# The last unit of a mixture-of-experts kernel holds two experts instead of one

## The chip, the cores and the metric

The kernel runs on one core of a Trainium2 chip. The metric is the device time of one execution in microseconds; the median of several runs counts.

## The reference

One decoder layer on 256 tokens of 1024 channels, all float32. First a token mixer (sparse attention and an mLSTM branch) with a residual and a LayerNorm, then a mixture of 16 experts, again with a residual and a LayerNorm. The change is in the experts:

```
def hier_moe(x, w_grp, b_grp, w_rt, b_rt, w_gate, w_up, w_down):
    t = x.reshape(-1, D)                                   # 256 x 1024
    ...                                                    # top group, then top 2 experts in it
    combine = ...                                          # 256 x 16, two nonzero weights per token
    out = jnp.zeros_like(t)
    for e in range(N_EXPERTS):                             # 16 experts
        hdn = jax.nn.silu(t @ w_gate[e]) * (t @ w_up[e])   # 1024 -> 512
        out = out + combine[:, e:e + 1] * (hdn @ w_down[e])  # 512 -> 1024
    return out.reshape(B, S, D)
```

## The kernel before

Up to about 228 us the kernel computes the token mixer, the first LayerNorm and the routing. Then come the experts, in seven units. The weights of an expert are 6 MB (gate, up and down, two halves of 1 MB each), 96 MB for all, and each is read once from HBM.

**Slots and units.** An expert does not compute all 256 tokens, only the tokens sent to it, up to a cap. Four experts have fixed slots with 64 columns each (`NSTAT`, `CAP`). The other twelve are sorted by their token counts on the chip, and `PLAN` (L30) gives their slots the widths 128; 64, 64; four times 32; four times 32; 32. A unit is one tuple of `PLAN`, 128 token rows in all, and `ORDER` (L31) is the order in which the units run after the two fixed ones: (64, 64), (32 x 4), (128), (32 x 4), (32). So the fifth unit is the expert with 128 columns, the sixth has four experts of 32 columns, and the seventh, the last one, has one expert of 32 columns (`ALONE`, L32). An expert with more tokens than its cap is finished by `beyond` (L1314), a branch with a loop that runs only if the counts ask for it.

**One unit.** `onehot` (L1093) builds a 0/1 matrix from tokens to columns for two units at once. `gather` (L1115) multiplies the normalised tokens, kept as a high and a low part in float32r, by it: for each of 8 chunks of channels four products with 128x128 stationary tokens and the one-hot as the moving operand, 256 columns for two units, 32 for the last one. `scaled` (L1110) takes the result out on ScalarE and VectorE. `back` (L1134) transposes the one-hot for the way back and picks the combine weights `cw`. `gate` (L1171), `up_h` (L1184) and `down` (L1236) are the three matrix products; the tokens are stationary, the weights move, 512 columns at a time. Where a unit has several experts, their columns lie in different column tiles of TensorE (`slots`, L1126: 2 x 64 or 4 x 32 columns), and the products of the experts run beside one another. A plain float32 product is two records in the trace, a float32r product is one. `hidden_T` (L1195) transposes the hidden values, `combine` (L1250) multiplies by the transposed one-hot and adds to `acc`.

**The last unit before.** Its one expert has 32 columns, so `product_alone` (L1151) puts four chunks of the contraction into the four column tiles, two deep, and a product with `fold` (a matrix that adds the four 32-row blocks and copies the sum to all four) gives the whole sum. `hidden_T` with `fold` does this for up. `down_part` (L1207) again has one quarter of the contraction in each column tile, one deep; the combine adds the four. The output columns are done in three parts (`CUTS`: 512, 320 and 192), and the last down half is loaded in the two smaller pieces (`late`).

**Order.** The main loop (L1410) emits for the third and the fifth unit: one-hot for two units, combine of an earlier unit, `back`, down product of the unit before, gather, gate, up, combine of the unit before; for the units between, which share that gather: `back`, gate, down product of the unit before, up. For the last unit it is: combine, `beyond`, one-hot, `back`, gather, down product of the sixth unit, gate, up, combine of the sixth unit, tail. A framework turns this into one program per engine; it moves independent instructions against one another, but not past the branch of `beyond`.

**Loads.** All weight loads stand in one list (`loads_in_order`, L302) in the order in which the units use them (for the last unit: down of the sixth, gate, up, down), and SP issues them in this order (`load`, L128). A load needs a free place of the ring `we`; `consumed` (L67) gives places back when a product has read them.

Of the kernel before, what the change touches and what calls it, by code (L numbers as in the profile page):

```python
# [17 lines left out]
P = 128  # L18
D = 1024
KC = D // P  # L20
S = 256
# [38 lines left out]
def tile_layer(ctx: ExitStack, tc: tile.TileContext, x, w_in, cst, rows, toep, w_uk, w_uv,  # L60
# [1072 lines left out]

    def back(OH, u, unit):  # L1134

        cm = unit[4]
        us = slice(u * P, (u + 1) * P)
        pt = tp_tile("poht")
        for b in range(NB):
            nc.tensor.transpose(pt[:, b * P:(b + 1) * P], OH[:, b, us].bitcast(F32), ident)  # L1140
        OHT = wk.tile([P, S], F32R, tag="sc", name="oht", bufs=2)
        nc.scalar.copy(OHT, pt[:, :S])  # L1142
        pc = sm_tile("pcw")
        for b in range(NB):
            nc.tensor.matmul(pc[:, 0:len(unit[1])], OH[:, b, us].bitcast(F32), cm[:, b, :], start=b == 0, stop=b == 1)
        cw = wk.tile([P, 1], F32, tag="cw", name="cw", bufs=2)
        for i, ss, _ in ((0, slice(0, P), {}),) if unit[2] == ALONE else slots(unit):
# [23 lines left out]
    def gate(unit, u, psg=None):  # L1171
        if unit[2] == ALONE:
            part = wk.tile([P, 512], F32, tag="w2", name="part", bufs=2)
            nc.scalar.copy(part, product_alone(unit, 0))
# [5 lines left out]
        sg = wk.tile([P, 512], F32, tag="w2", name="sg", bufs=2)  # L1180
        nc.scalar.activation(sg, psg, AF.Silu)
        return sg

    def up_h(unit, u, sg, cw):  # L1184
        if unit[2] == ALONE:
            psu = product_alone(unit, 1)
# [3 lines left out]
        h = wk.tile([P, 4, P], F32, tag="w2b", name="h", bufs=2)  # L1190
        nc.vector.scalar_tensor_tensor(h.rearrange("p j q -> p q j"), psu.rearrange("p (q j) -> p q j", j=4), cw[:, 0:1],  # L1191
# [3 lines left out]
    def hidden_T(h, alone=False):  # L1195
        pt = tp_tile("pht").rearrange("p (j t) -> p j t", j=4)
        for j in range(4):
            if alone:

                nc.tensor.matmul(pt[:, j, :], h[:, j, :], fold, start=True, stop=True)  # L1200
            else:
                nc.tensor.transpose(pt[:, j, :], h[:, j, :], ident)
        hT = wk.tile([P, 4, P], F32, tag="hT", name="hT")
# [3 lines left out]
    def down_part(unit, hT, y, c0, n):  # L1207
# [12 lines left out]
    def y_parts(y, psd, c0, n):  # L1220
        ys = slice(c0, c0 + n)
        nc.scalar.copy(y[:, 0, ys], psd)  # L1222
        nc.vector.tensor_tensor(y[:, 1, ys], psd, y[:, 0, ys].bitcast(F32), op=ALU.subtract)  # L1223
# [12 lines left out]
    def down(unit, h):  # L1236
        hT, y = hidden_T(h), y_tile()
# [76 lines left out]
    def beyond():  # L1314

        assert not pend
        n_more = nc.values_load(nex[0:1, 0:1], min_val=0, max_val=2 * NE, skip_runtime_bounds_check_because="a sum of counts")
        item = wk.tile([P, 1], F32, tag="nmx", name="item")
        nc.gpsimd.memset(item, 0.0)
        with tc.If(n_more > 0):  # L1320
            with tc.For_i(0, n_more, 1):
# [31 lines left out]
                nc.vector.tensor_scalar(item, item, 1.0, None, op0=ALU.add)  # L1353

# [5 lines left out]
    def others():  # L1360
# [39 lines left out]
        fold_xg = wk.tile([P, P + KC * 32], F32, tag="wrs", name="fold_xg")  # L1400
        fold = fold_xg[:, :P]
        xga = fold_xg[:, P:].rearrange("p (k t) -> p k t", k=KC)
        nc.vector.tensor_reduce(fold[:, 0:32], ident.rearrange("p (i s) -> p s i", i=4), AX.X, ALU.add)
        nc.vector.tensor_copy(fold[:, 32:].rearrange("p (i s) -> p i s", i=3), fold[:, 0:32].unsqueeze(1).to_broadcast([P, 3, 32]))
        return fold, xga
# [4 lines left out]
    for n in range(NUNITS):  # L1410
        unit = units[n]
        if waits:
            if unit[2] == ALONE:
# [3 lines left out]
            if unit[2] != ALONE:  # L1417
                combine(*waits)
        OHT, cw = back(OH, n % 2, unit)
        if waits and unit[2] == ALONE:  # L1420
            gather(OH, 32, xg=xga)
        if waits:
            y = down(*prev[:2])
            if unit[2] != ALONE:
                gather(OH, 2 * P)
# [3 lines left out]
        if n == 1:  # L1429
            fold, xga = others()  # L1430
# [102 lines left out]
```

## Time and profile before

| | |
|---|---|
| median of 3 runs | 445.21 us (442.96 to 446.66) |
| the profiled execution | 442.91 us |
| its span, first to last instruction | 441.2 us |
| granted TensorE clock, mean | 0.974 |
| busy: TensorE, VectorE, ScalarE, GpSimd | 95%, 51%, 37%, 10% |
| read from HBM | 135.74 MB, 310 GB/s over the span |

The profiled execution is 1.7 us longer than its span. Busy shares are means over stages with different limits: the mixer with many small steps, and the experts with TensorE and the DMA engines both busy. In the trace PE is a matrix product on TensorE and PEld its weight load, DVE is VectorE, ACT is ScalarE, POOL is GpSimd, SPq is the queue of the engine that issues the loads. `psg`, `psu`, `pp` and `psd` are the results of gate, up, the last unit's gate and up, and down; `pxg` is the gather; `poht` and `pht` are transposes, `pcomb` the combine.

### The profile page before, as it was taken

How to read it: one execution, taken by the hardware profiler on the slowest of the kernel's cores; microseconds unless marked ns; L12 is line 12 of the kernel's file. 1: busy time of each engine (PE TensorE's matmuls, PEld its weight loads, DVE VectorE, ACT ScalarE, POOL GpSimd, SP SyncE). 2: the span in 40 equal slices, each digit the busy share in tenths (PEclk: the TensorE clock that was granted, in tenths of full speed). 3: DMA queues.
4: the chain of work that ended last, by engine and by line, in shares of the span. 5: the costliest groups of instructions: out<-in, count | busy, mean ns of one | idle time of the engine just before them, and what ended most of it. 6: DMA issues, size and time to landing. Idle time of an engine off the chain costs nothing.

```text
span 441.2 us, 7257 instructions
## 1 busy us (share of the span) xinstructions
PE 417.0 (95%) x2832; PEld 300.9 (68%) x2832; DVE 226.1 (51%) x493; ACT 163.3 (37%) x294; POOL 45.4 (10%) x74
## 2 busy tenths in 40 slices
PE   6999999999999999999999999999998999979980
PEld 6999996999999999999974345443334444436340
DVE  3698996499656755686573118214031212221247
ACT  4558556766766444455465020210112100101210
POOL 6325305031011001110000000000000000000001
PEclk9999999999999999999999999999999999995995
DMA  8982770797296788659697999999999999999972
GB/s 254 340 271 83 282 247 4 232 377 231 113 362 215 283 271 302 190 179 386 229 352 284 359 424 420 403 377 426 422 420 423 418 424 420 423 419 420 415 253 95
DMA packets 48518, 137.28 MB, mean 311 GB/s; under 512 B 3538, under 2 KB 32354, under 8 KB 36450
## 3 DMA queue, kind: packets, MB, share of 16 engines
q1 hardware_dynamic: 47394, 135.75, 81.1%
q10 hardware_dynamic: 1088, 1.05, 0.8%
q8 instruction: 23, 0.38, 0.4%
q14 instruction: 13, 0.11, 0.1%
HBM read 135.74 MB, written 1.05 MB: 310 GB/s over the span
## 4 chain that ended last, share of the span: by engine, by line
PE 80%; DMA 10%; DVE 5%; ACT 3%; issue 1%; SPq 0%; POOL 0%; DVEq 0%; ACTq 0%
PE psg L1166 10%; PE psu L1166 9%; PE psd L1243 7%; PE accT L253 7%; PE accT L249 7%; PE accT L252 7%; DMA we<-in_w_gate_dram 4%; DMA we<-in_w_down_dram 4%; PE pcomb L1229 3%; PE pxg L1121 2%; PE accY L249 2%; PE accZ L249 2%; PE accK L249 2%; PE accK L252 2%; PE accK L253 2%; PE accZ L253 2%
## 5 line engine op out<-in xcount | busy, mean ns | idle before, releaser
L249 PE MATMUL accT<-xh,split 128*128 128x256 f32 (+1 forms) x264 | 75.6, 286 | 0.0
L253 PE MATMUL accT<-xh,split 128*128 128x256 f32 (+1 forms) x264 | 75.1, 284 | 0.3 <-DVE split L240 0.3
L252 PE MATMUL accT<-xl,split 128*128 128x256 f32 (+1 forms) x264 | 75.1, 284 | 0.0
L240 DVE TENSOR_TENSOR split<-raw,split 128x1024 fp32r<-128x1024 f32 (+2 forms) x52 | 63.9, 1234 | 18.5 <-ACT split L239 18.3
L239 ACT CAST split<-raw 128x1024 fp32r<-128x1024 f32 (+2 forms) x59 | 59.3, 1013 | 32.4 <-PE accT L253 9.8
L1243 PE MATMUL psd<-we,hT 128*32 128x512 f32 (+2 forms) x240 | 48.6, 634 | 1.9 <-ACT hT L1204 1.9
L253 PEld LDWEIGHTS accT<-xh,split 128*128 128x128 f32 (+1 forms) x264 | 50.1, 190 | 0.5 <-DVE split L240 0.5
L249 PEld LDWEIGHTS accT<-xh,split 128*128 128x128 f32 (+1 forms) x264 | 50.1, 190 | 0.4 <-PE pl L589 0.2
L252 PEld LDWEIGHTS accT<-xl,split 128*128 128x128 f32 (+1 forms) x264 | 50.1, 190 | 0.0
L1166 PE MATMUL psu<-we,xg 128*32 128x512 f32 (+2 forms) x240 | 47.5, 594 | 0.0
L1166 PE MATMUL psg<-we,xg 128*32 128x512 f32 (+2 forms) x232 | 45.8, 595 | 0.0
L1223 DVE TENSOR_TENSOR y<-psd,y 128x512 fp32r<-128x512 f32 x12 | 8.3, 692 | 64.6 <-ACT y L1222 64.6
L1243 PEld LDWEIGHTS psd<-we,hT 128*32 128x32 f32 (+2 forms) x240 | 15.5, 131 | 30.4 <-issue 25.3
L1166 PEld LDWEIGHTS psu<-we,xg 128*32 128x32 f32 (+2 forms) x240 | 15.2, 126 | 26.7 <-issue 26.4
L1166 PEld LDWEIGHTS psg<-we,xg 128*32 128x32 f32 (+2 forms) x232 | 13.9, 125 | 24.4 <-issue 22.6
L1191 DVE SCALAR_TENSOR_TENSOR h<-psu,cw,sg 128x512 f32<-128x512 f32 x6 | 6.7, 1120 | 46.1 <-PE psu L1166 33.5
L1472 POOL TENSOR_TENSOR nm<-nm,nhalf 128x2 f32<-128x2 f32 x1 | 1.8, 1771 | 209.5 <-DVE nm L1473 209.5
L1222 ACT CAST y<-psd 128x512 fp32r<-128x512 f32 x12 | 7.0, 586 | 40.6 <-PE psd L1243 40.6
L1230 DVE TENSOR_TENSOR x<-x,pcomb 128x512 f32<-128x512 f32 (+2 forms) x30 | 17.9, 645 | 7.4 <-PE pcomb L1229 7.3
L1142 ACT CAST oht<-poht 128x256 fp32r<-128x256 f32 x7 | 2.6, 372 | 50.6 <-PE pcomb L1229 32.0
L240 POOL TENSOR_TENSOR split<-raw,split 128x1024 fp32r<-128x1024 f32 x7 | 17.5, 2501 | 20.1 <-ACT split L239 19.9
L1229 PE MATMUL pcomb<-y,oht 128*128 128x512 f32 (+2 forms) x60 | 18.6, 436 | 0.2 <-ACT y L1217 0.2
(356 smaller groups left out, 811.3 us busy)
## 6 DMA issues: line engine op xcount, KB each, us to landing
we<-in_w_up_dram SPq DMA_DIRECT2D x32, 1024.0 KB, 10.1
we<-in_w_gate_dram SPq DMA_DIRECT2D x31, 1024.0 KB, 9.5
we<-in_w_down_dram SPq DMA_DIRECT2D x31, 1024.0 KB, 13.5
raw<-in_w_in_dram SPq DMA_DIRECT2D x18, 1024.0 KB, 6.9
raw<-in_w_out_dram SPq DMA_DIRECT2D x4, 1024.0 KB, 4.9
raw<-in_w_up_a_dram SPq DMA_DIRECT2D x2, 1024.0 KB
raw<-in_w_up_m_dram SPq DMA_DIRECT2D x2, 1024.0 KB, 6.0
raw<-in_w_in_dram SPq DMA_DIRECT2D x2, 528.0 KB
```

The lines of the kernel that those rows point to most:

```text
L239: a = nc.scalar.copy(hi, raw)
L240: b = (nc.gpsimd if pool else nc.vector).tensor_tensor(lo, raw, hi.bitcast(F32), op=ALU.subtract)
L249: i = nc.tensor.matmul(o, ah, bh, start=start, stop=False)
L252: nc.tensor.matmul(o, ah, bl, start=False, stop=False)
L253: return nc.tensor.matmul(o, al, bh, start=False, stop=stop)
L1121: nc.tensor.matmul(ps[:, k, :n], part[:, b, (k0 + k) * P:(k0 + k + 1) * P], OH[:, b, :n], start=i == 0, stop=i == 3)
L1166: last = nc.tensor.matmul(ps[ss, :], xg[:, kc, u * P + ss.start:u * P + ss.stop], wtiles[unit[0], wi, i, hf][kc % 4], start=kc == 0, stop= ...
L1222: nc.scalar.copy(y[:, 0, ys], psd)
L1223: nc.vector.tensor_tensor(y[:, 1, ys], psd, y[:, 0, ys].bitcast(F32), op=ALU.subtract)
L1229: i = [nc.tensor.matmul(pc, o, v, start=i == 0, stop=i == len(parts) - 1) for i, (o, v) in enumerate(parts)]
L1230: nc.vector.tensor_tensor(acc[:, b, ys], acc[:, b, ys], pc, op=ALU.add)
L1243: nc.tensor.matmul(psd[nh][ss, :], hT[:, j, ss], wtiles[unit[0], 2, i, hf][j % 2][:, nh * 512:nh * 512 + 512], start=j == 0, stop=j == 3, ...
```

## The change

`PLAN` becomes 128; 64, 64; four times 32; three times 32; 32, 32. The caps of the twelve slots stay as they were, but the sixth unit now has three experts and the last one two (`PAIR`). In the last unit each expert gets two column tiles: its 32 columns stand twice in the one-hot, and each tile takes every other chunk of the contraction, four deep for gate and up and two deep for down. `fold` adds the two blocks of an expert. The last gather has 64 columns, the two copies left out, and writes the common `xg` instead of a tile of its own; it still stands ahead of the sixth unit's down product. Since the sixth unit has only 96 rows, the gather of units five and six has 224 moving columns instead of 256, and its tiles are cut to 96 rows. Two experts' down weights now come in column halves and in the two small pieces. When `beyond` is reached, all but two places of the ring hold weights that are still needed, so its loop takes turns on two places.

```diff
-PLAN = ((128,), (64, 64), (32, 32, 32, 32), (32, 32, 32, 32), (32,))
+PLAN = ((128,), (64, 64), (32, 32, 32, 32), (32, 32, 32), (32, 32))
-ALONE = (32,)
+PAIR = (32, 32)
...
-            if ws == ALONE:
+            if ws == PAIR:
                 for b in range(NB):
-                    nc.vector.tensor_scalar(OH[:, b, :P].rearrange("p (e j) -> p e j", e=4), iota1[:, :32].unsqueeze(1).to_broadcast([P, 4, 32]),
-                                            pm[:, b, 0:1], None, op0=ALU.is_equal)
+                    for i in range(2):
+                        nc.vector.tensor_scalar(OH[:, b, i * 64:i * 64 + 64].rearrange("p (e j) -> p e j", e=2),
+                                                iota1[:, :32].unsqueeze(1).to_broadcast([P, 2, 32]), pm[:, b, i:i + 1], None, op0=ALU.is_equal)
...
-    def gather(OH, n, kcs=range(KC), xg=xg):
+    def gather(OH, n, kcs=range(KC), twice=False):
+        def of(b):
+            return OH[:, b, :2 * n].rearrange("p (e i j) -> p e i j", e=2, i=2)[:, :, 0, :] if twice else OH[:, b, :n]
...
-                    nc.tensor.matmul(ps[:, k, :n], part[:, b, (k0 + k) * P:(k0 + k + 1) * P], OH[:, b, :n],
+                    nc.tensor.matmul(ps[:, k, :n], part[:, b, (k0 + k) * P:(k0 + k + 1) * P], of(b),
...
+    def rows_of(unit):
+        return P if unit[2] == PAIR else sum(unit[2])
...
-    def product_alone(unit, wi):
+    def product_pair(unit, wi):
         pp = acc_tile("pp")
         for hf in range(2):
-            for k in range(4):
-                t = slice(k * 32, k * 32 + 32)
-                nc.tensor.matmul(pp[t, :], xga[:, hf * 4 + k, :], wtiles[unit[0], wi, 0, hf][k], start=hf == 0, stop=hf == 1,
-                                 tile_position=(0, k * 32))
-            consumed(1)
+            for k in range(0, 4, 2):
+                for i in range(2):
+                    for r in range(2):
+                        t = i * 64 + r * 32
+                        nc.tensor.matmul(pp[t:t + 32, :], xg[:, hf * 4 + k + r, i * 32:i * 32 + 32], wtiles[unit[0], wi, i, hf][k + r],
+                                         start=hf * 4 + k == 0, stop=hf * 4 + k == 6, tile_position=(0, t))
+            consumed(2)
         return pp
...
-        for j in range(4):
-            t = slice(j * 32, j * 32 + 32)
-            i = nc.tensor.matmul(psd[t, :], hT[:, j, t], wtiles[unit[0], 2, 0, nh][j][:, o:o + n], start=True, stop=True, tile_position=(0, j * 32))
-            first = first or i
+        for j in range(0, 4, 2):
+            for e in range(2):
+                for r in range(2):
+                    q = e * 64 + r * 32
+                    i = nc.tensor.matmul(psd[q:q + 32, :], hT[:, j + r, q:q + 32], wtiles[unit[0], 2, e, nh][j + r][:, o:o + n],
+                                         start=j == 0, stop=j == 2, tile_position=(0, q))
+                    first = first or i
...
     def beyond():
+        kept = rings["we"], turn["we"]
+        rings["we"], turn["we"] = (place("we"), place("we")), 0
...
+        rings["we"], turn["we"] = kept
...
-            if unit[2] == ALONE:
+            if unit[2] == PAIR:
                 combine(*waits)
                 beyond()
...
-        if waits and unit[2] == ALONE:
-            gather(OH, 32, xg=xga)
+        if waits and unit[2] == PAIR:
+            gather(OH, 64, twice=True)
         if waits:
             y = down(*prev[:2])
-            if unit[2] != ALONE:
-                gather(OH, 2 * P)
+            if unit[2] != PAIR:
+                gather(OH, P + rows_of(units[n + 1]))
```

Left out are the places where 128 rows become `rows_of(unit)`, the two copies into `cw`, and the new `fold`, two additions of blocks of the identity.

## Rows read from the trace of the kernel before

**Rows 1.** The page's section 2: the span in 40 equal slices of 11.03 us. A digit is the busy share in tenths; the last line is what the DMA engines moved.

```profile
PE   6999999999999999999999999999998999979980
DMA  8982770797296788659697999999999999999972
GB/s 254 340 271 83 282 247 4 232 377 231 113 362 215 283 271 302 190 179 386 229 352 284 359 424 420 403 377 426 422 420 423 418 424 420 423 419 420 415 253 95
```

**Rows 2.** The DMA queue's own waits (SP) from 340 us to the end: who was waited for, us in total, times, longest.

```profile
SPq L130 <- DMA we<-in_w_up_dram: 19.4, 10, 1.9
SPq L130 <- DMA we<-in_w_gate_dram: 15.4, 8, 2.2
SPq L130 <- DMA we<-in_w_down_dram: 15.0, 8, 2.0
...
SPq L130 <- PE psg L1166: 0.7, 2, 0.4
...
SPq L130 <- PE psu L1166: 0.3, 1, 0.3
```

**Rows 3.** The DMA view from 340 us to the end: GB/s in 40 slices of 2.55 us, and issues by line with size and median us from issue to landing.

```profile
GB/s 424 418 411 427 418 431 414 414 424 421 437 411 414 421 421 431 414 424 418 431 421 405 421 418 424 418 424 418 431 418 396 379 314 323 88 0 0 0 364 47
...
we<-in_w_down_dram SPq DMA_DIRECT2D x11, 1024.0 KB, 19.8
...
lnr<-in_rows_dram SPq DMA_DIRECT2D x2, 512.0 KB, 4.4
...
we<-in_w_down_dram SPq DMA_DIRECT2D x1, 384.0 KB, 17.4
```

**Rows 4.** The timeline of the last unit: start in us, length, engine, line, what it is, and in brackets the idle time before it with what ended that.

```profile
413.10 1.21 PE L1157 MATMUL pp<-we,fold_xg 128*32 128x512 f32 x8
...
414.80 1.06 PE L1157 MATMUL pp<-we,fold_xg 128*32 128x512 f32 x8 [0.49 <-DMA we<-in_w_gate_dram]
...
415.95 0.59 ACT L1174 COPY part<-pp 128x512 f32<-128x512 f32 x1 [1.89 <-PE pp L1157]
...
416.82 1.02 PE L1176 MATMUL psg<-part,fold_xg 128*128 128x512 f32 x2
...
417.77 1.06 PE L1157 MATMUL pp<-we,fold_xg 128*32 128x512 f32 x8
...
419.77 1.07 PE L1157 MATMUL pp<-we,fold_xg 128*32 128x512 f32 x8 [0.93 <-SPq L1320]
...
420.96 1.14 DVE L1191 SCALAR_TENSOR_TENSOR h<-pp,cw,sg 128x512 f32<-128x512 f32 x1 [3.12 <-issue]
...
424.04 1.60 PE L1215 MATMUL psd<-we,hT 128*32 128x512 f32 x16 [0.73 <-ACT hT L1204]
...
425.81 1.98 PE L1229 MATMUL pcomb<-y,oht 128*128 128x512 f32 x4 [0.17 <-ACT y L1217]
```

**Rows 5.** The same timeline from the sixth unit's up product to the end of its down product; the first row is the issue of the down loads by SP.

```profile
380.03 10.28 SPq L130 DMA_DIRECT2D we<-in_w_down_dram  x5
...
394.98 0.48 DVE L1100 TENSOR_SCALAR oh<-iota,pmP 128x128 fp32r<-128x128 f32 x2 [0.32 <-DVEq L1320]
...
395.41 0.43 PE L1140 MATMUL poht<-ident,oh 128*128 128x128 f32 x2 [1.88 <-DVE oh L1100]
...
397.02 0.18 PE L1121 MATMUL pxg<-oh,x1h 128*128 128x32 f32 x1 [0.60 <-issue]
...
397.05 0.26 PE L1121 MATMUL pxg<-oh,x1l 128*128 128x32 f32 x1
...
397.16 0.26 PE L1121 MATMUL pxg<-oh,x1h 128*128 128x32 f32 x1
...
398.62 0.37 PE L1121 MATMUL pxg<-oh,x1l 128*128 128x32 f32 x1
...
398.84 0.37 PE L1121 MATMUL pxg<-oh,x1h 128*128 128x32 f32 x1
...
404.09 9.35 PE L1243 MATMUL psd<-we,hT 128*32 128x512 f32 x64 [0.73 <-ACT hT L1204]
```

**Rows 6.** Windows of 10 us: stretch, its length, busy time of PE, PEld, DVE, ACT and POOL with counts, the mean granted TensorE clock, the DMA share, GB/s.

```profile
394.00:404.00 10.00, 7.35 (x42) 6.99 (x42) 2.53 (x8) 2.43 (x6) 0.00 (x0) 0.71 1.02 418
404.00:414.00 10.00, 9.91 (x72) 3.42 (x72) 0.69 (x1) 1.15 (x3) 0.00 (x0) 0.78 1.02 423
```

**Rows 7.** The timeline of VectorE at the end: the first add of the last combine, the aggregate (11 instructions lie between, in line), and one of the smallest instructions.

```profile
426.98 0.69 DVE L1230 TENSOR_TENSOR x<-x,pcomb 128x512 f32<-128x512 f32 x1 [3.77 <-PE pcomb L1229]
...
432.27 0.36 DVE L1470 BATCH_NORM_AGGREGATE mv<-bst 128x2 f32<-128x18 f32 x2
...
432.74 0.16 DVE L1473 TENSOR_SCALAR nm<-mv 128x2 f32<-128x2 f32 x1
```

**Rows 8.** Timelines of TensorE: two products of the gather of 256 columns, and products over two column tiles, one tile and four tiles.

```profile
279.82 4.03 PE L1243 MATMUL psd<-we,hT 128*64 128x512 f32 x18
...
336.03 0.28 PE L1121 MATMUL pxg<-oh,x1l 128*128 128x256 f32 x1
336.15 0.28 PE L1121 MATMUL pxg<-oh,x1h 128*128 128x256 f32 x1
...
379.69 3.60 PE L1243 MATMUL psd<-we,hT 128*128 128x512 f32 x8
...
386.36 7.16 PE L1166 MATMUL psu<-we,xg 128*32 128x512 f32 x62
```

More of the change, by code (lines that the diff above doesn't have):

```diff
@@ L1132, in slots @@
             q += w
+    def rows_of(unit):
+        return P if unit[2] == PAIR else sum(unit[2])
     def back(OH, u, unit):
-        cm = unit[4]
-        us = slice(u * P, (u + 1) * P)
+        cm, r = unit[4], rows_of(unit)
+        us = slice(u * P, u * P + r)
         pt = tp_tile("poht")
         for b in range(NB):
-            nc.tensor.transpose(pt[:, b * P:(b + 1) * P], OH[:, b, us].bitcast(F32), ident)
-        OHT = wk.tile([P, S], F32R, tag="sc", name="oht", bufs=2)
-        nc.scalar.copy(OHT, pt[:, :S])
+            nc.tensor.transpose(pt[:r, b * P:(b + 1) * P], OH[:, b, us].bitcast(F32), ident)
+        OHT = wk.tile([P, S], F32R, tag="sc", name="oht", bufs=2)[:r]
+        nc.scalar.copy(OHT, pt[:r, :S])
         pc = sm_tile("pcw")
         for b in range(NB):
-            nc.tensor.matmul(pc[:, 0:len(unit[1])], OH[:, b, us].bitcast(F32), cm[:, b, :], start=b == 0, stop=b == 1)
+            nc.tensor.matmul(pc[:r, 0:len(unit[1])], OH[:, b, us].bitcast(F32), cm[:, b, :], start=b == 0, stop=b == 1)
         cw = wk.tile([P, 1], F32, tag="cw", name="cw", bufs=2)
-        for i, ss, _ in ((0, slice(0, P), {}),) if unit[2] == ALONE else slots(unit):
+        for i, ss, _ in [(i, slice(i * 64, i * 64 + 64), {}) for i in range(2)] if unit[2] == PAIR else slots(unit):
             nc.vector.tensor_copy(cw[ss, :], pc[ss, i:i + 1])
         return OHT, cw
-    def product_alone(unit, wi):
+    def product_pair(unit, wi):
         pp = acc_tile("pp")
         for hf in range(2):
-            for k in range(4):
-                t = slice(k * 32, k * 32 + 32)
-                nc.tensor.matmul(pp[t, :], xga[:, hf * 4 + k, :], wtiles[unit[0], wi, 0, hf][k], start=hf == 0, stop=hf == 1,
-                                 tile_position=(0, k * 32))
-            consumed(1)
+            for k in range(0, 4, 2):
[5 more added lines that the diff above has]
+            consumed(2)
         return pp
@@ L1171, in gate @@
     def gate(unit, u, psg=None):
-        if unit[2] == ALONE:
+        if unit[2] == PAIR:
             part = wk.tile([P, 512], F32, tag="w2", name="part", bufs=2)
-            nc.scalar.copy(part, product_alone(unit, 0))
+            nc.scalar.copy(part, product_pair(unit, 0))
             psg = acc_tile("psg")
@@ L1179, in gate @@
             product(psg, unit, 0, u)
-        sg = wk.tile([P, 512], F32, tag="w2", name="sg", bufs=2)
-        nc.scalar.activation(sg, psg, AF.Silu)
+        sg = wk.tile([P, 512], F32, tag="w2", name="sg", bufs=2)[:rows_of(unit)]
+        nc.scalar.activation(sg, psg[:rows_of(unit)], AF.Silu)
         return sg
     def up_h(unit, u, sg, cw):
-        if unit[2] == ALONE:
-            psu = product_alone(unit, 1)
+        if unit[2] == PAIR:
+            psu = product_pair(unit, 1)
         else:
@@ L1189, in up_h, with hidden_T @@
             product(psu, unit, 1, u)
[L1190 to L1191 removed]
+        r = rows_of(unit)
+        h = wk.tile([P, 4, P], F32, tag="w2b", name="h", bufs=2)[:r]
+        nc.vector.scalar_tensor_tensor(h.rearrange("p j q -> p q j"), psu[:r].rearrange("p (q j) -> p q j", j=4), cw[:r, 0:1],
                                        sg.rearrange("p (q j) -> p q j", j=4), op0=ALU.mult, op1=ALU.mult)
         return h
[L1195 to L1196 removed]
+    def hidden_T(h, pair=False):
+        r = h.shape[0]
+        pt = tp_tile("pht").rearrange("p (j t) -> p j t", j=4)[:, :, :r]
         for j in range(4):
[L1198 removed]
+            if pair:
                 nc.tensor.matmul(pt[:, j, :], h[:, j, :], fold, start=True, stop=True)
             else:
[L1202 to L1203 removed]
+                nc.tensor.transpose(pt[:, j, :], h[:, j, :], ident[:r, :r])
+        hT = wk.tile([P, 4, P], F32, tag="hT", name="hT")[:, :, :r]
         nc.scalar.copy(hT, pt)
@@ L1236, in down @@
     def down(unit, h):
-        hT, y = hidden_T(h), y_tile()
+        hT, y = hidden_T(h), y_tile()[:rows_of(unit)]
         psd = [acc_tile("psd") for _ in range(2)]
@@ L1398, in others @@
                         nc.vector.scalar_tensor_tensor(acc[:, b, ns], pgb, ALPHA, acc[:, b, ns], op0=ALU.mult, op1=ALU.add)
[L1400 to L1405, printed above, removed]
+        fold = wk.tile([P, P], F32, tag="wrs", name="fold")
+        fv, iv = (t.rearrange("p (e r j) -> p e r j", e=2, r=2) for t in (fold, ident))
+        for r in range(2):
+            nc.vector.tensor_tensor(fv[:, :, r, :], iv[:, :, 0, :], iv[:, :, 1, :], op=ALU.add)
+        return fold
     units = list(first)
@@ L1412, in tile_layer @@
         if waits:
-            if unit[2] == ALONE:
+            if unit[2] == PAIR:
                 combine(*waits)
@@ L1429, in tile_layer @@
         if n == 1:
-            fold, xga = others()
+            fold = others()
         h = up_h(unit, n % 2, sg, cw)
```

7 lines of the change are left out of this document (4 added, 3 removed).

## The prediction

> **What bounds the kernel now.** I read the 40 slices first [rows 1]: from the 24th slice on the DMA engines are full at about 420 GB/s, and TensorE is busy too, so the page does not say which of the two is in front. The DMA queue's own waits settle what paces the transfers [rows 2]: after 340 us SP waits for the landing of earlier loads (19.4 + 15.4 + 15.0 us) and almost never for TensorE to free a place (0.7 + 0.3 us). A load takes some 20 us from issue to landing, several in flight [rows 3]. So the weights arrive at their own pace: the second gate half and the second up half of the last expert are waited for at 414.80 and 419.77 us [rows 4], and with 2 MB between them that is 2.49 us per MB.
>
> TensorE's own path runs beside it. The sixth unit's up product ends at 393.5 us [rows 8]; then one-hot, transposes, gather, `pht` and the sixth unit's down product follow in line until 413.1 us [rows 5]. In that stretch the mean granted clock is 0.71 and then 0.78 [rows 6]: a product of the gather begins 0.11 us after the one before it ahead of 398 us and 0.21 us after it later [rows 5], the two levels of 2.4 and 1.2 GHz. At 413.1 the paths meet. Without transfers TensorE would go straight on; it waits 0.84 us ahead of 414.80 (two steps of 0.43 after 413.10 would be 413.96) and 1.14 us ahead of 419.77 (two steps after 417.77) [rows 4]. Behind the last `hT` (424.0 us) come the down parts, the `y` copy, the combine, and 5.3 us of VectorE without a gap up to the aggregate at 432.27 [rows 4, 7]. So the end hangs on a transfer path and a TensorE path that lie within about 1 us of each other.
>
> **Part by part.** (1) *Order of loads.* The last unit now owns 12 of the 96 loads, not 6, and gate, up and down come at the end in this order. Its last gate load becomes number 88 instead of 92, its last up load 92 instead of 94. At 2.49 us per MB they land at about 404.8 and 414.8 us. The sixth unit's down loads end at number 84 instead of 90: the last of them, issued at 390.0 us and landed 19.8 us later [rows 3, 5], comes 15 us earlier. So no gate or up weight of the last unit is waited for. The price: 4 MB instead of 2 come as column pieces with short rows, and the rate over these falls from 420 to 314 and 323 GB/s [rows 3]; I estimate at most 1 us at the end of the transfers (425 to 426 us). The last piece is first needed by part 2's product, behind the first combine, so this costs nothing. Two more DMA issues cost nothing either, in a queue that waits for landings. The constants `lnr2` still go out when SP has passed the overflow branch; they land 4.4 us after 422.6 [rows 3], 6 us ahead of their use.
>
> (2) *Sixth unit with three experts.* A product over four 32-column tiles goes in steps of four records: 62 records take 7.16 us, 15 steps of 0.43 and the last record's length, and a stall of about 0.1 to 0.3 us. One tile (8 records in 3.60 us) and two (18 in 4.03) go at 0.43 us a step too [rows 8]. Three experts need the same eight steps per product, so TensorE gains nothing; the trace has no three-tile step, and I take 0.43.
>
> (3) *Gather of units five and six, 224 columns instead of 256.* Each of the 32 products takes 0.12 us at 256 columns [rows 8]; the trace has none between 32 and 256 columns. From below: 0.11 us, as at 32 columns (0.3 us gained in all). From above: the rate of a plain f32 product, two records of 0.43 us for 512 columns, which makes 0.37 us for 224 columns, 32 x 0.25 = 8.1 us more. The 32-column gather lies outside in width but shows the rate: at 397.02 a product begins, and the next begins at 397.05 [rows 5], where the f32 rate would need 0.05 us. Nearest in width is 256. I take 0.12: nothing.
>
> (4) *Last gather, 64 columns (each half twice in the one-hot) instead of 32.* 32 products as before; 64 columns at the f32 rate are 0.107 us, no more than the spacing that 32 columns have now. Nothing. The one-hot is four VectorE instructions of 64 columns instead of two of 128, which take 0.48 us together [rows 5]; the smallest VectorE instruction takes 0.16 [rows 7], so this is 0.2 to 0.5 us more, on the path: 0.3. The stall of part (2) disappears with the earlier landings. These two cancel.
>
> (5) *Products of the last unit.* Gate: eight steps for four, from 413.10: the last step begins at 413.10 + 7 x 0.43 = 416.1 instead of 414.80 + 0.43 = 415.2, so 0.9 us later although the wait is gone. `part`, the fold product and the start of up move by 0.9, to 418.65. Up: the last step begins at 418.65 + 3.0 = 421.65 instead of 420.2, now 1.45 late. `h`, `pht` and `hT` keep their durations and move by 1.45.
>
> (6) *Down parts.* Part 0 has four steps for two (+0.86), part 1 four of 0.27 us for two (+0.53), and both stand ahead of the first combine product. `hT` at 425.5, then 1.72 + 1.07: the combine begins at 428.3 instead of 425.81, +2.5 us. VectorE's chain behind it has no gap that takes this up, so the aggregate, the last normalisation and the output move by 2.5 us. Part 2 (+0.3) lies beside VectorE's work.
>
> (7) The doubled `fold`, a second `cw` copy (under the gather, 6 us), evictions of 96 rows instead of 128 and the overflow branch's two places (its body has no record in the trace) cost nothing on the path.
>
> Sum: +2.5 us on the profiled execution's 442.91, so 445.4. That execution is at the fast end of the runs before (median 445.21, 442.96 to 446.66); what lengthens the others is not shown. Were it the transfers, the new order has 5 us of slack for it; were it TensorE, it stays. I carry half of the 2.3 us: **446.6 us**.
>
> **Rivals.** *A: the 224-column gather goes at the f32 rate.* It lies on TensorE's path at 335 to 344 us, and transfers that are early cover nothing behind it: 446.6 + 8.1 = 454.7, the slow side. It passes one per cent as soon as a product costs more than about 0.22 us. Against it stands the 0.03 us spacing; for it, that this is a single pair of rows.
>
> *B: the clock does not fall at 398 us.* The means of 0.71 and 0.78 over 10 us each [rows 6] are 2.9 + 2.2 us of lost time, of which I count 4.5, since some of it is waiting. In the kernel before, this would win nothing: loads at 409.8, 414.8 and 419.8 us hold TensorE. Now it counts: 442.1. For it, the gather streams twice the columns; against it, the same idle 1.9 us ahead of the transposes [rows 5].
>
> *C: a step of three tiles is longer.* If the tiles of one step don't close up with the next, a step takes a record's whole 0.59 us (3.60 less seven steps [rows 8]): 24 steps by 0.16 are 3.9 us, 450.5. For it, that no such step is in the trace; against it, that one, two and four tiles agree. The Trainium skill ("TensorE: Matmul & The Clock Gate", section "Measured speedup vs the span model") gives three column tiles a speedup of only 2.38; by that figure this would be an estimated 2.7 us instead, and no run here shows it.
>
> *D: early weights let the program's order put gate steps into TensorE's idle time*, 2.65 of the 10 us from 394 [rows 6], and the clock stays up: 446.6 - 4.5 - 2.65 = 439.5. Against it, the code emits down ahead of gate.
>
> **How the numbers follow.** Forecast 0.59, A 0.17, B 0.12, C 0.05, D 0.07. The forecast's own range is 443.5 to 449.7 (how long the low clock lasts, about 2 us, and where the median falls). Leaving out D and little else, the range goes from 441.5 (under B) to 456 (over A). One per cent, 4.45 us, is about what a measurement of this kernel can tell from no change. Faster by that (under 440.8): D and a sliver of B, 0.08. Slower (over 449.7): A, most of C, a tail of the forecast of 0.05: 0.26. Within: 0.66.
>
> **What would show it.** Right: no wait for a transfer ahead of the last unit's `pp` products, eight steps 0.43 us apart from about 413 us, `h` near 422.4, first combine near 428.3, transfers ending at about 426 as before, three-expert steps of 0.43 us. Wrong: `pxg` products of 224 columns over 0.2 us apart (A), a granted clock of 1.00 from 394 to 414 us (B), longer steps in the sixth unit (C), `pp` products ahead of the down product (D).

## The result and the profile after

The changed kernel takes 450.08 us (median of 3 runs, 448.73 to 451.64) against 445.21 us: a ratio of 1.0143 [1.0108, 1.0178]. The time lies within the stated range of 441.5 to 456 us, but 3.5 us over the forecast of 446.6 and outside the forecast's own range of 443.5 to 449.7; the step that moved it was not among the forecast's terms or its rivals. Its profiled execution has a span of 448.4 us where the kernel before has 441.2, so the 7.2 us between the two traces can be followed.

Most of them arise ahead of the last unit's products. This is the timeline of TensorE in the kernel **after**, the fourth unit's down product (`psd`, four experts on four column tiles) and two of the gather's products; between the rows of `psd` lie the products of the gather for units five and six.

```profile
334.71 0.66 PE L1213 MATMUL pht<-ident,h 128*128 128x128 f32 x4 [1.23 <-DVE h L1201]
...
336.09 1.92 PE L1258 MATMUL psd<-we,hT 128*32 128x512 f32 x8 [0.51 <-ACT hT L1215]
...
338.26 0.27 PE L1124 MATMUL pxg<-oh,x1h 128*128 128x224 f32 x1
338.37 0.28 PE L1124 MATMUL pxg<-oh,x1l 128*128 128x224 f32 x1
...
339.02 1.90 PE L1258 MATMUL psd<-we,hT 128*32 128x512 f32 x4
...
341.94 3.62 PE L1258 MATMUL psd<-we,hT 128*32 128x512 f32 x20
...
346.01 1.90 PE L1258 MATMUL psd<-we,hT 128*32 128x512 f32 x4
...
348.48 1.90 PE L1258 MATMUL psd<-we,hT 128*32 128x512 f32 x4
...
351.50 3.65 PE L1258 MATMUL psd<-we,hT 128*32 128x512 f32 x24
```

The same stretch in the kernel **before**:

```profile
335.18 0.66 PE L1202 MATMUL pht<-ident,h 128*128 128x128 f32 x4 [1.22 <-DVE h L1191]
...
336.56 1.92 PE L1243 MATMUL psd<-we,hT 128*32 128x512 f32 x8
...
341.64 1.90 PE L1243 MATMUL psd<-we,hT 128*32 128x512 f32 x4
...
344.48 7.05 PE L1243 MATMUL psd<-we,hT 128*32 128x512 f32 x52
```

Both do the same 64 records (32 matmuls, two records each). Before, they come in three pieces, 1.92 + 1.90 + 7.05 = 10.87 us; after, in six, 14.89 us. The lengths tell why. Records begin in steps 0.43 us apart, and a step takes that long whether one record begins in it or four on four column tiles. A piece is its steps and a last record of 0.59 us: four steps for the pieces of 1.9 us, eight for those of 3.6, sixteen for the one of 7.05. The piece of four records (two matmuls) spends its four steps on one record each. So the product takes 4 + 4 + 16 = 24 steps before and 4 + 4 + 8 + 4 + 4 + 8 = 32 after. Eight more steps are 3.4 us, and each of the three more pieces has the rest of a last record, 0.16 us and a little more: 4.0 us in all. The large piece is not full either: four tiles would do 64 records in sixteen steps, and it does 52; its last four records begin one by one. The gather's products themselves go at the old rate: 0.11 us from one to the next at 224 columns. From the start of `pht` to the end of the product it is 4.1 us longer: 334.71 to 355.15 us where before it was 335.18 to 351.53.

The source of neither product was changed. The order in which TensorE gets them is not written in the code either; it is chosen when the program is built, and as TensorE ran it the fourth unit's down product is cut into 4, 2, 26 matmuls before and 4, 2, 10, 2, 2, 12 after.

The rest comes at the end, where the prediction looked. The timeline from the sixth unit's up product on, in the kernel **after**:

```profile
390.03 7.06 PE L1175 MATMUL psu<-we,xg 128*32 128x512 f32 x46
...
408.24 9.30 PE L1258 MATMUL psd<-we,hT 128*32 128x512 f32 x45 [0.62 <-ACT hT L1215]
...
417.37 0.60 PE L1258 MATMUL psd<-we,hT 128*32 128x512 f32 x3
...
417.41 3.99 PE L1166 MATMUL pp<-we,xg 128*32 128x512 f32 x31
...
421.48 0.58 ACT L1183 COPY part<-pp 128x512 f32<-128x512 f32 x1 [2.87 <-PE pp L1166]
...
423.31 3.64 PE L1166 MATMUL pp<-we,xg 128*32 128x512 f32 x32
...
427.08 1.13 DVE L1201 SCALAR_TENSOR_TENSOR h<-pp,cw,sg 128x512 f32<-128x512 f32 x1 [3.70 <-issue]
...
430.15 3.00 PE L1228 MATMUL psd<-we,hT 128*32 128x512 f32 x32 [0.73 <-ACT hT L1215]
...
433.08 1.98 PE L1244 MATMUL pcomb<-y,oht 128*128 128x512 f32 x4
...
439.53 0.35 DVE L1487 BATCH_NORM_AGGREGATE mv<-bst 128x2 f32<-128x18 f32 x2
```

Neither `pp` product waits for a transfer any more: the waits of [rows 4] ahead of 414.80 and 419.77 us are gone. Against the same points of [rows 4, 5, 7, 8], the sixth unit's up product ends 3.57 us later (397.09 for 393.52), its down product starts 4.15 us later, `part` 5.53, `h` 6.12, the first combine 7.27, the aggregate 7.26. VectorE's chain gives nothing back.

The granted clock in the kernel **after** (stretch, its length, PE busy, granted clock, DMA share, GB/s), and then **before**:

```profile
394.00:400.00 6.00, 3.93 (x29) 1.00 1.01 415
400.00:413.60 13.60, 12.98 (x58) 0.50 1.01 416
```

```profile
392.00:398.00 6.00, 3.52 (x32) 1.00 1.01 418
398.20:408.20 10.00, 9.27 (x45) 0.50 1.01 418
```

Both begin at 1.00 (2.4 GHz) and fall to 0.50 (1.2 GHz) with the gather of the last unit under way. The lower level lasts 13.6 us where it lasted 10. From the end of the sixth unit's up product to the start of the last step of its down product 0.58 + 0.55 = 1.13 us are lost. The 0.55 lie in the down product, which has 5.4 us at the lower level where it had 4.3. The 0.58 ahead of it are a balance: the one-hot takes 0.74 us instead of 0.48 and more of the gather is at the lower level, but TensorE's pause of 0.60 us [rows 5] is gone, and the transposes of three experts are shorter than those of four.

So the 7.27 us at the first combine are: 3.57 at the end of the sixth unit's up product (4.09 at the fourth unit's down product, less a start that was 0.47 earlier, and 0.05 less by then), 1.13 in the stretch around the half clock, 0.83 in gate, 0.59 in up, 1.15 in the down parts.

### The profile page after: what moved, and what is told of

It reads as the page before. It is cut to its first block, busy times and chain, and to the rows that moved or that the text cites. A ratio compares the mean times of both kernels' runs of the same rounds, so it can differ in the third digit from the quotient of the medians.

```text
span 448.4 us, 7283 instructions
## 1 busy us (share of the span) xinstructions
PE 426.6 (95%) x2840; PEld 301.3 (67%) x2840; DVE 226.4 (50%) x495; ACT 163.4 (36%) x294; POOL 45.4 (10%) x74
## 3 DMA queue, kind: packets, MB, share of 16 engines
q10 hardware_dynamic: 1088, 1.05, 0.8%
HBM read 135.74 MB, written 1.05 MB: 305 GB/s over the span
## 5 line engine op out<-in xcount | busy, mean ns | idle before, releaser
L1258 PE MATMUL psd<-we,hT 128*32 128x512 f32 (+2 forms) x224 | 53.0, 636 | 2.3 <-ACT hT L1215 2.3
L1238 DVE TENSOR_TENSOR y<-psd,y 128x512 fp32r<-128x512 f32 (+1 forms) x12 | 8.3, 690 | 61.4 <-ACT y L1237 61.4
L1201 DVE SCALAR_TENSOR_TENSOR h<-psu,cw,sg 128x512 f32<-128x512 f32 (+1 forms) x6 | 6.7, 1122 | 46.4 <-PE psu L1175 33.6
L1149 ACT CAST oht<-poht 128x256 fp32r<-128x256 f32 (+1 forms) x7 | 2.6, 371 | 50.9 <-PE pcomb L1244 32.0
L1237 ACT CAST y<-psd 128x512 fp32r<-128x512 f32 (+1 forms) x12 | 7.0, 585 | 37.7 <-PE psd L1258 37.7
L1114 DVE TENSOR_SCALAR xg<-pxg,cst_sb 128x256 f32<-128x256 f32 (+2 forms) x14 | 6.7, 477 | 25.6 <-ACT xg L1113 25.6
L240 POOL TENSOR_TENSOR split<-raw,split 128x1024 fp32r<-128x1024 f32 x7 | 17.4, 2496 | 21.1 <-ACT split L239 13.6
```

Source lines behind the costliest of these rows:

```text
L240: b = (nc.gpsimd if pool else nc.vector).tensor_tensor(lo, raw, hi.bitcast(F32), op=ALU.subtract)
L1114: nc.vector.tensor_scalar(xg[:, k + 1, :n], odd, ln1gq[:, k + 1:k + 2], ln1bq[:, k + 1:k + 2], op0=ALU.mult, op1=ALU.add))
L1237: nc.scalar.copy(y[:, 0, ys], psd[:r])
L1238: nc.vector.tensor_tensor(y[:, 1, ys], psd[:r], y[:, 0, ys].bitcast(F32), op=ALU.subtract)
L1258: nc.tensor.matmul(psd[nh][ss, :], hT[:, j, ss], wtiles[unit[0], 2, i, hf][j % 2][:, nh * 512:nh * 512 + 512], start=j == 0, stop=j == 3, ...
```

## The experiments

Each was timed beside the kernel before on the same chip; ratios are to that. That took 443.75 us beside experiments 1, 3, 4 and 5, 443.11 us beside 7, 8, 9 and 11, and 443.61 us beside 2, 6 and 10.

**1. The gather at 256 columns again.** All else stays as changed; the last 32 columns of the one-hot are a copy of the 32 ahead of them (two instructions of VectorE, left out in the diff).

```diff
...
-                gather(OH, P + rows_of(units[n + 1]))
+                gather(OH, 2 * P)
```

> The changed kernel, with the common gather of units five and six 256 columns wide again (columns 224 to 255 repeat the last expert's one-hot and are not read). Theory 1 (order): the framework's static order of TensorE in units four and five is then that of the kernel before, and the pieces of the fourth unit's down product that run on one column tile alone shrink from four to one or two; that stretch is 4.0 us shorter and the whole kernel is 4 us faster than the changed one, about 446 us, ratio to before about 1.003 to 1.006. Theory 2 (cover): the 4 us at 335 to 355 us are taken back by waits for transfers in the last two units, and the loss lies in the last unit's longer products alone; then about 449 to 450 us, ratio 1.013.

444.67 us, 1.003 [1.0009, 1.0052]. `psd` of the fourth unit in this run:

```profile
336.45 1.92 PE L1261 MATMUL psd<-we,hT 128*32 128x512 f32 x8
...
341.53 1.90 PE L1261 MATMUL psd<-we,hT 128*32 128x512 f32 x4
...
344.38 7.05 PE L1261 MATMUL psd<-we,hT 128*32 128x512 f32 x52
...
427.55 1.98 PE L1247 MATMUL pcomb<-y,oht 128*128 128x512 f32 x4
```

The wider gather, which does more, brings the three pieces of before back, and with them 5.0 us of the change's loss (1.43% less 0.3% of 445 us). The first combine is 1.74 us behind that of [rows 4] and 5.53 ahead of the changed kernel's. Of these 5.53, 3.87 are there at the end of the sixth unit's up product (393.22 for 397.09); the other 1.67 come in the stretch behind it, where the lower clock lasts 10.2 us here (397.6 to 407.9) and 13.6 in the changed kernel. So the new order also cost through the clock; why the lower level lasts longer there no run shows.

**2. The narrow gather alone, in the kernel before.** The sixth unit's fourth expert gets no gathered rows; no instruction is left out.

```diff
-                gather(OH, 2 * P)
+                gather(OH, 2 * P - (32 if n == 4 else 0))
```

> The kernel before the change with one edit: the gather for units five and six takes 224 columns, not 256. The sixth unit's fourth expert is left without its gathered rows (that part of the computation is left out); every instruction stays, 32 of them with 224 columns. It does one part of the change alone. Theory, the narrower gather alone changes the order of TensorE's instructions: the fourth unit's down product is cut into pieces of 4, 2, 10, 2, 2 and 12 matmuls, and TensorE is about 4 us later at the end of that product (355 us for 351.5). In this kernel transfers cover part of it: the waits of 0.84 us and 1.14 us ahead of the last unit's second gate and up halves go first, and 2.2 to 3.3 us are left at hT: 445.5 to 446.6 us beside a kernel before of 443.3, ratio 1.005 to 1.0075. Rival, the 4 us come from another part of the change (three experts, the one-hot, the loads): ratio 1.000, and the fourth unit's down product ends at 351.5 us.

445.72 us, 1.0048 [1.003, 1.0066].

```profile
337.59 1.92 PE L1243 MATMUL psd<-we,hT 128*32 128x512 f32 x8 [0.51 <-ACT hT L1204]
...
340.52 1.90 PE L1243 MATMUL psd<-we,hT 128*32 128x512 f32 x4
...
343.44 3.62 PE L1243 MATMUL psd<-we,hT 128*32 128x512 f32 x20
...
347.51 1.90 PE L1243 MATMUL psd<-we,hT 128*32 128x512 f32 x4
...
349.98 1.90 PE L1243 MATMUL psd<-we,hT 128*32 128x512 f32 x4
...
353.00 3.65 PE L1243 MATMUL psd<-we,hT 128*32 128x512 f32 x24
```

The same six pieces, from the width alone. With experiment 1 this settles the cause: the width orders the pieces, in both kernels. The price is smaller here, 2.1 us, since the waits for transfers in the last unit take up part of it, as expected; 2.2 to 3.3 us were forecast.

**3. The down product in one piece.** In the changed kernel, 224 columns, the gather ahead of the whole of the fourth unit's down product, whose matmuls are chained in order.

```diff
...
-            y = down(*prev[:2])
-            if unit[2] != PAIR:
-                gather(OH, P + rows_of(units[n + 1]))
+            g = lambda: gather(OH, P + rows_of(units[n + 1]))
+            y = down(*prev[:2], g if n == 4 else None)
+            if n == 2:
+                g()
```

> The changed kernel with 224 columns, but the gather of units five and six is put ahead of the whole down product of the fourth unit, which then runs in steps of four tiles without a break. Theory 1: TensorE needs about 4.6 us for the gather and 7.1 us for the product instead of 19.8 us for both, so it is 8 us early; since the last unit waits for no transfer, nearly all of it arrives at the end: 442 to 443 us, ratio about 0.993. Theory 2: waits for transfers take it back, about 449 us.

444.05 us, 0.9995 [0.9973, 1.0017]: the 1.4% are gone, but no more; the theory's 0.993 was not reached. The gather and the product end 12.5 us behind the end of `pht` (336.77 to 349.31), 7.2 us less than in the changed kernel and 3.2 less than in the kernel before, which takes 15.7 (335.84 to 351.53). About a third of the 3.2 is lost at once to another small piece, in the sixth unit's gate, where the order now puts two pieces of one matmul ahead of the count and transpose products:

```profile
365.03 1.04 PE L1177 MATMUL psg<-we,xg 128*32 128x512 f32 x2
366.00 0.50 PE L1154 MATMUL pcw<-pmP,oh 128*96 128x3 f32 x4
366.43 1.04 PE L1177 MATMUL psg<-we,xg 128*32 128x512 f32 x2
367.41 0.66 PE L1215 MATMUL pht<-ident,h 128*128 128x128 f32 x4
```

**4. The same in the kernel before.** The edit of experiment 3 with 256 columns.

> The kernel before, with its gather of 256 columns put ahead of the whole down product of the fourth unit in the same way. TensorE is some 3.8 us early there. Theory 1 with the two paths of the prediction: the loads that land at 410, 414.8 and 419.8 us hold TensorE, so the kernel gains at most 0.5 to 1 us, ratio 0.997 to 1.0. Rival: transfers were never in the way and 3.8 us arrive, ratio 0.991.

443.66 us, 1.0000 [0.9974, 1.0025]. TensorE is 3 us early at the end of the product (348.57) and then waits in the sixth unit's up product:

```profile
384.57 4.48 PE L1168 MATMUL psu<-we,xg 128*32 128x512 f32 x34
389.63 1.04 PE L1168 MATMUL psu<-we,xg 128*32 128x512 f32 x2 [0.58 <-DMA we<-in_w_up_dram]
392.13 3.62 PE L1168 MATMUL psu<-we,xg 128*32 128x512 f32 x26 [1.46 <-DMA we<-in_w_up_dram]
```

These 3 us of TensorE are worth nothing in the kernel before: its weights come no sooner. (The traced execution took 445.16 us, more than the median, so the waits may be long in it.)

**5. Less half clock.** The kernel of experiment 3, with ten products of the identity (2.50 us) behind the overflow branch, where TensorE waits for the one-hot.

```diff
...
+        if waits and unit[2] == PAIR:
+            pw_ = sm_tile("warm4")
+            for i in range(10):
+                nc.tensor.matmul(pw_[:, :P], ident, ident, start=True, stop=True)
         OHT, cw = back(OH, n % 2, unit)
```

> As the run with the whole down product on the changed kernel, and ten float32 products of the identity (128 columns, result unused) directly behind the overflow branch, where TensorE waits 1.9 us for the one-hot. If TensorE's idle time there is what lets the clock fall, the granted clock stays 1.0 through gather and down product and 3 to 4 us more are won, about 439 us, until the last loads (about 426 us) hold the end. If the narrow products of the gather let it fall, the clock falls all the same and the time is that of the run without them, or up to 1 us more.

443.12 us, 0.9985 [0.9966, 1.0005], not to be told from experiment 3. The lower level is short in this run (400.9 to 404.3 us), and the last `hT` is used at 421.46, 2.2 us earlier than in experiment 3 (423.63). But 1.1 of these are there already at the fourth unit's `pht` (335.02 for 336.11), far ahead of the edit. The dummies bring only the other 1.1, since they also push the transpose of the one-hot back: it begins 3.7 us behind the end of the sixth unit's up product, against 2.0 us in experiment 3. Then the second piece of the last down weights is waited for, issued at 410.74 us and landed 13.6 us later:

```profile
421.46 2.45 PE L1230 MATMUL psd<-we,hT 128*32 128x512 f32 x20 [0.73 <-ACT hT L1217]
...
424.39 1.27 PE L1230 MATMUL psd<-we,hT 128*32 128x320 f32 x12 [0.48 <-SPq L1345]
425.59 1.98 PE L1246 MATMUL pcomb<-y,oht 128*128 128x512 f32 x4
```

Transfers are what comes next, and they take the dummies' share back: the first combine is 1.0 us earlier than in experiment 3 (426.56), no more than `pht` was. So the time is that of the expectation's second case: the clock falls all the same, if for a shorter time.

**6. Dummy products with the order of before.** Experiments 1 and 5 together.

> The kernel after the change with the gather 256 wide (444.67 us alone, half clock for 10.3 us from 397.6 us) and ten dummy products behind the branch, in TensorE's idle time. It tells what the half clock costs without the broken order. Theory, the half clock lasts about 3.4 us, so TensorE comes 3.4 us earlier to hT (421.2 us for 424.6), and the second 640 KB piece, which lands at about 424 us, takes part of it back: the first combine near 425.4, 442 to 442.7 us, ratio 0.997 to 0.998. Rival, the half clock is not shortened or not on the path: 444.7 us, ratio 1.003.

444.69 us, 1.0033 [1.0018, 1.0049]: the time of experiment 1, and the theory missed. The lower level did get shorter (6.8 us for 10.2), but the dummies stand in the way of what they were to help: the transpose of the one-hot (`poht`) comes at 396.99 us instead of 395.27. This experiment:

```profile
394.66 2.50 PE L1442 MATMUL warm<-ident 128*128 128x128 f32 x20 [1.38 <-DVEq L1340]
396.99 0.38 PE L1150 MATMUL poht<-ident,oh 128*128 128x128 f32 x2
```

Experiment 1:

```profile
395.27 0.56 PE L1150 MATMUL poht<-ident,oh 128*128 128x128 f32 x2 [2.05 <-DVE oh L1101]
```

The first combine comes at 427.62 for 427.55.

**7. Half the steps in the last unit.** Experiment 1 with every second contraction step of the last gate and up left out.

```diff
-            for k in range(0, 4, 2):
+            for k in (0,):
...
```

> The kernel after the change with the gather 256 wide (its time alone: 444.67 us, first combine at 427.55 us), and in the last unit's gate and up only every second contraction step: half of that unit's contraction is left out. All loads stay. It tests part 5 of the prediction by itself. Theory, TensorE's steps of the last unit are on the path since its weights are early: four steps of 0.43 us fewer in the gate and four in up, 3.4 us earlier at hT; the first down part can then begin near 421.2 us, the second 640 KB piece lands at about 424 us and takes part of this back, so the first combine comes 2 to 2.5 us earlier than with all steps, and the time is about 442.3 us, 0.5% under the 444.67. Rival, transfers hold the last unit as they did in the kernel before: hT stays where it is, and the time is that of the kernel with all steps, within 0.5 us.

442.66 us, 0.9991 [0.9976, 1.0006], 0.4% under experiment 1, as forecast. `hT` is used at 421.44 for 424.62, the first combine comes at 425.19 for 427.55, 2.4 us earlier; the first two down parts take 3.82 us, not 3.00, since the second piece, landed at 423.9, is waited for. The last unit's steps lie on the path, up to the point where that transfer takes over.

**8. The tail in another order.** Experiment 5 with each part's combine directly behind that part.

```diff
-        if i == 0:
-            last_part(0)
-        if i + 1 < len(CUTS):
-            last_part(i + 1)
+        last_part(i)
```

> The kernel of the run before (the fourth unit's down product in one piece and ten dummy products behind the branch; 443.12 us, 0.9985 of the time before), with each down part's combine directly behind that part, not behind the next part. Theory, the first combine waits for no second part: the second part of the down product (four steps of 0.27 us and its wait for the 640 KB piece, 1.5 us together) is no longer ahead of the first combine product, which comes at about 424.1 us, not 425.6; VectorE's chain follows, about 441.5 us, ratio 0.995. Rival, the chain of VectorE's work is then held by the later parts, whose y copies and combines now alternate with its own instructions: the aggregate stays, ratio 0.998 to 1.000.

443.13 us, 1.0006 [0.9986, 1.0027]. The first combine does come at 424.07, 1.5 us earlier, and the aggregate at 432.14 for 432.03. The theory's 0.995 was not reached, and the rival holds: VectorE now waits 0.69 and 0.54 us for the later parts.

**9. Whole steps in the sixth unit too.** Experiment 8, with three or six matmuls of the sixth unit's gate and up (whole steps) ahead of the products that were put between them.

> As the run with the combine directly behind each part, and the sixth unit's gate and up are issued in whole steps of three tiles around the count, transpose and combine products (three or six products ahead of these, where the order had one). Theory, no lone-tile piece is left in the sixth unit, so TensorE reaches the last unit's gate 1 to 2 us earlier, but the last down pieces still land at 424 to 426 us: at most 1 us better than without this, 440.5 to 441.5 us, ratio 0.992 to 0.995. Rival, transfers set the end already: the same time within 0.3 us, and a longer wait of TensorE for the second piece, over 1.5 us.

441.69 us, 0.9971 [0.9957, 0.9985], the fastest of all, 8.4 us under the changed kernel and 0.3% under the one before. Neither forecast fits: it is 1.4 us under experiment 8, more than the theory's 1 us, but its ratio is above 0.995. TensorE reaches the last unit's gate 1.45 us earlier (406.79 for 408.24), and is then early enough to wait for weights again:

```profile
413.15 2.77 PE L1168 MATMUL pp<-we,xg 128*32 128x512 f32 x20
416.80 1.91 PE L1168 MATMUL pp<-we,xg 128*32 128x512 f32 x12 [0.88 <-DMA we<-in_w_up_dram]
```

The traced execution took 443.44 us, the longest of the twelve; in experiment 10, whose traced execution is near its median (442.35 us), this wait is 0.30 us.

**10. Experiment 9 with the old tail.**

> The kernel with whole steps everywhere and dummy products (441.69 us, 0.9971), with the tail in the order of the kernel before (the next part ahead of each combine). Theory, transfers hold the last unit and both orders of the tail end within 0.3 us of each other: ratio 0.996 to 0.998. Rival, the gaps that the other order left in VectorE's chain (0.69 us ahead of the third part's adding, 0.5 us ahead of the last) were the price of its earlier first combine, and without them the end is 0.5 to 1 us earlier: ratio 0.9945 to 0.996.

442.65 us, 0.9979 [0.9956, 1.0001]: the two orders of the tail can't be told apart, as the theory had it. The second down part waits 1.20 us for its weights here.

**11. The edits of experiment 8 in the kernel before.**

> The kernel before the change, with the same three edits as far as it has their places: the fourth unit's down product in one piece, ten dummy products behind the branch, each part's combine directly behind the part. It tells what the edits are worth without the change. Theory, transfers hold the last unit's gate and up there (the second up half lands at about 420 us whatever TensorE does), so the first two edits bring nothing, and the third at most the second part's time, 0.5 to 1 us: ratio 0.998 to 1.000. Rival, TensorE held the kernel before too: 442 us or less, ratio 0.995.

444.70 us, 1.0047 [1.0025, 1.0068]. Nothing is gained, as the theory said, but the half per cent that it loses was not expected. In the traced execution (443.36 us, the shortest of its runs) the tail is longer: from the first combine to the aggregate 7.2 us (425.54 to 432.75) for 6.46 in [rows 4, 7]. What the rest of the loss is stays open.

## Why the prediction was right or wrong

**What bounds the kernel: right, with a new place.** The kernel before is held by transfers (experiment 4), and the change takes that hold off the last gate and up. TensorE's path then sets the end, as forecast.

**Part 1, order of loads: right.** No `pp` product waits, and the last weights land at 425.6 us (425 to 426 was forecast): the last piece is issued at 416.38 us, and the DMA view gives its size and its time to landing.

```profile
we<-in_w_down_dram SPq DMA_DIRECT2D x1, 384.0 KB, 9.2
```

This is what the DMA engines moved from 340 us on, in slices of 2.55 us:

```profile
GB/s 424 421 421 418 421 421 427 421 418 418 434 418 421 421 408 434 421 421 414 418 434 424 414 411 431 414 424 405 397 386 377 361 288 203 251 5 0 0 0 0
```

The two slices from 424 to 429 us, some 1.2 MB, are for the most part the constants `lnr`, 1 MB issued from 424.06 us on. SP's queue shows a wait that was not there before [rows 2], 5.8 us that the profile puts down to the sixth unit's `pht`. The first two rows of SP's waits from 340 us on, and that one, in the kernel after:

```profile
SPq L130 <- DMA we<-in_w_gate_dram: 15.7, 9, 2.1
SPq L130 <- DMA we<-in_w_down_dram: 15.5, 8, 2.0
...
SPq L130 <- PE pht L1213: 5.8, 1, 5.8
```

It made no weights late: in the kernel before, without it, the last piece lands at 425.2 us. In the changed kernel TensorE uses these pieces later still, from 430.15 us on; once TensorE came earlier, the second of them was what it waited for (experiments 5, 7, 10).

**Part 2, three experts: right.** 46 records of the sixth unit's up take 7.06 us where 62 took 7.16 [rows 8], and three tiles begin together every 0.43 us. Rival C is out. It was also counted too small: a product of the sixth unit has sixteen steps, as part 2's fifteen and a last record say, so gate, up and down have 48 and not 24, and C would have cost 7.7 us, not 3.9. The figure of 2.38 for three column tiles that the Trainium skill gives ("TensorE: Matmul & The Clock Gate", section "Measured speedup vs the span model") is not borne out by this trace: here a step of three tiles takes as long as a step of one, 0.43 us.

**Part 3, the gather: the step that failed.** It priced the 32 products at their own rate, and that was right: 0.11 us each, rival A is out. "I take 0.12: nothing" did not ask what else a shorter product changes. The order on TensorE is chosen when the program is built, and the width of this tile changes it; by what rule, no run here shows. The fourth unit's down product, which no line of the change touches, fell into small pieces and took 4.1 us more of TensorE; in time it cost 5.0 us (experiment 1), partly through the longer half clock. What a small piece costs could be read in the trace before: the piece of four records at 1.90 us stands there between gather products. What could not be read there was that the new order would have three more small pieces; that takes the built program. Experiments 1 and 2 show it from both sides.

**Parts 4 and 7:** the longer one-hot is there (0.74 us for four instructions, 0.26 more than before; 0.3 was forecast), and the stall of the sixth up product did not return. Nothing of either decided.

**Part 5: right.** 0.9 was forecast for gate and 0.83 measured; 1.45 at `h`, measured 0.83 + 0.59 = 1.42. Experiment 7 shows that these steps are on the path.

**Part 6: right.** 1.05 us forecast behind `hT`, 1.15 measured.

**The clock:** the forecast kept the half clock's length and gave it some 2 us in its own range. It grew from 10 to 13.6 us, and the stretch around it cost 1.13. Rival B, no half clock, did not happen in any run. In experiment 5, where it lasted 3.4 us, the last down pieces took the gain back, so B's 4.5 us would hardly have arrived whole; how much of them would, no run shows.

**Rival D**, gate steps in TensorE's idle time, did not come about, but its thought was the right one at the wrong place: it asked whether the built order would be another, and only for the last unit.

The sum: forecast 2.5 us and half of 2.3 for the median. Measured in the trace 7.27: 2.57 for parts 5 and 6, 1.13 in the stretch around the half clock, 3.57 order. With the order of before (experiment 1) the ratio is 1.003, 1.3 us, close to what was forecast for the whole. There parts 5 and 6 cost what they should, and 0.8 us come back ahead of them, since TensorE reaches the last step of the sixth unit's down product earlier than before (411.83 for 412.67). The slower result, which had been given 0.26, mostly for rivals A and C, came by neither. That 450.08 still lies within the stated range is luck: its upper end of 456 was there for A.

## What to carry to other kernels

Where the order of instructions is chosen when the program is built, a change of one tile's width may re-order products that it does not touch: compare the built order of every engine before and after, and look for products over several column tiles that have been cut into pieces shorter than one step. Chain such a product's matmuls in whole steps if it matters. And ask of each repair which transfer is late next: experiments 5, 7, 9 and 10 each ended in a wait for weights of the last unit.

## What the runs showed of the hardware that was not expected

- Two matmuls (four records) whose records begin one by one take 1.90 us; 60 records that share their steps take 7.06 us (the fourth unit's down product in experiment 4), 0.12 each.
- A product of the gather takes as long at 224 columns (0.11 us) as at 32 [rows 5] and nearly as at 256 (0.12).
- The clock fell in the last two units in every run. In the kernel after it fell at 400.0 us, as the gather began, 2.9 us behind the end of the sixth unit's up product; in the one before at 398.1, in the middle of the gather, 4.6 us behind it. With 2.5 us of identity products ahead of the gather, which leave 1.4 us idle, it fell at 400.9 (experiment 5) and 400.8 (experiment 6), 9.7 and 7.5 us behind the up product, and stayed down for 3.4 and 6.8 us.
